# A decoder trunk on one Trainium2 core: tile addresses, a store queue, and the order of exponentials and scores

## The chip, the cores and the metric

The kernel runs on one core of one Trainium2 chip. The metric is the device time of one execution in microseconds (us), median of the runs shown. The core's engines run side by side, each in the order of its own queue: TensorE (PE in the profile, with PEld for its weight loads), VectorE (DVE), ScalarE (ACT), GpSimd (POOL) and SyncE (SP). They share the on-chip memories SBUF and PSUM. Transfers are issued by SP, ScalarE or POOL, each with a queue of its own, and carried out by 16 DMA engines.

## The reference, cut to what matters

A trunk of one layer over 512 tokens and 16 leading meta tokens, in float32. Two branches mix the tokens: causal pooling over four windows, and a Mamba-2 state-space branch (SSD) with 8 groups of 4 heads. Sigmoid gates merge them, and an MLP with a squared ReLU follows.

```python
proj = u @ w_in[i]                      # u = rmsnorm(h); columns: pool, z, xbc, dt, gates
xbc = jax.nn.silu(causal_depthwise_conv(xbc, conv_w, conv_b))
...
a_cs = jnp.cumsum(a_dt, axis=2)
lmat = jnp.exp(jnp.where(mask, a_cs[:, :, :, None] - a_cs[:, :, None, :], -jnp.inf))
cb = jnp.einsum("bclgn,bcsgn->bclsg", cf, bf)
y_diag = jnp.einsum("bclsg,bclsgr,bcsgrp->bclgrp", cb, lmat, xdt)
states = jnp.einsum("bclgn,bclgr,bclgrp->bcgrpn", bf, decay_states, xdt)
...
y_off = jnp.einsum("bclgn,bcgrpn,bclgr->bclgrp", cf, prev, jnp.exp(a_cs))
...
y_ssd = mamba2_branch(z, xbc, dt_raw, ...) @ w_ssd_out[i]
h = h + (gate_pool * y_pool + gate_ssd * y_ssd) @ w_o[i]
hid = jax.nn.relu(rmsnorm(h, mlp_norm_w[i]) @ w_ff1[i])
h = h + (hid * hid) @ w_ff2[i]
out = rmsnorm(h, final_norm_w)[:, N_META:]
```

The inputs are x, the meta tokens and the layer's weights; the output is 512 x 1024.

## The kernel before, in words

**Precision.** Every large product is computed as three products of halves: an operand is split into a high part (a rounding copy) and a low part (the rest), and hi·hi, hi·lo and lo·hi are summed in PSUM. A weight block of 128 x 1024 is loaded by SP into a tile `raw`, copied by ScalarE into `whi` (L94) and subtracted by VectorE into `wlo` (L96). `raw` has 3 buffers, `whi` and `wlo` have 4, all in the pool `wp`. Tiles whose names end in h and l are such halves: `uh`, `ul` of the normalised input, `yh`, `yl` of the SSD's result, `yph`, `ypl` of the pooling's, `vsh`, `vsl`, `vh`, `vl` and `hh`, `hl` in the MLP.

**Stages.** Up to some 70 us: the norm, group 0's projections and four gates. To some 500 us: a loop over the 8 groups g. Then the pooling branch (to some 560 us), the remaining gates with the merge and `w_o` (to some 700), and the MLP. Some products are computed by a scheme with seven products of quarter blocks in place of eight (`pair`, tiles `pqx`; in the pooling stage `pxx`, `py` and `pz` at L978; in the MLP `px` and `alpha`), which needs sums of weight blocks.

**The group loop.** In turn g the generator `ssd(g)` is woven with generators that fill PE's time: `group_proj(g + 1)` (the next group's projections), in turn 4 also `out_half` (the first half of the SSD's output projection, tiles `pso`), in turn 7 `out_part` (`psp`), and `weight_sums_at`.

`group_proj` makes, in this order, the projections for B and C (`px{g}_{16+g}`, `px{g}_{24+g}`), for the two halves of x (as `px{g}_{2g}` and `px{g}_{2g+1}`, or for the groups in `X_PAIRS`, 4 to 7, as one `pqx{g}`), a gate in some turns (`gate_pool`), and z (`pz`). `conv` turns a projection into the tile `bt`, `ct` or `xc`: a bias step on ScalarE that reads PSUM (L414), three steps on VectorE (L416, L417) and a silu on ScalarE (L419). PSUM has two buffers for the wide tiles and four for the small ones, so a projection waits for the bias step that frees its buffer. So `px7_23` is the projection for B of group 7, the first of the next group while `ssd(6)` runs.

`ssd(g)` is this: POOL loads `abc`, the running sums of the group broadcast over partitions (L572, issued on POOL's queue). PE transposes B into `ptb`, which ScalarE copies to `btok` (L581), and x into `ptm` and `ptx`, from which VectorE makes `xddm`, `xdt` and `xdd`. ScalarE takes the exponential of `abc` into `eb` in two halves (L603), and ScalarE and VectorE subtract and clip (L608 the ScalarE part); `decay` takes the exponentials of the rest (L614, L615). PE makes the scores `pcb` (L625), which VectorE masks into `cbm`, and the states `pst` (L632, L634) from `btok`. ScalarE copies the first state to `st` (L636), VectorE chains the others. VectorE multiplies the decays by the masked scores. PE makes `po` from `st` (L654) and `py` from the decays (L660). The result is normalised (`png`, `rs` at L681) and split into `yh` and `yl` (L690).

**Stores.** `gate_pool` writes gates 0 to 6 to DRAM (`gate_d`, L719) and `out_half` writes its sums (`acc_d`, L798); both are read back in the merge. They are issued on POOL's queue, as the load of `abc` and the weight sums are.

**Weight sums.** `weight_sums_at` forms sums of weight blocks by transfers alone, on POOL's queue, which add into DRAM: eight transfers in a set of `fx` or `f1`, four in one of `f2`. Ahead of each step POOL copies one element into `seen`, a 128 x 1 tile whose only purpose is to hold the step back until a certain point of the computation (`mark`). `SETS_AT` says how many sets run in each turn of the loop, `SETS_POOL` how many in the pooling stage; what is left runs at the start of the MLP. The sets are taken from one list in a fixed order, among them f1's third set (f12), f2's third and fourth (f22, f23), f1's fourth (f13) and f2's fifth (f24), in this order.

**What sets the order.** A scheduler orders each engine's instructions as the program is built, with costs of its own. `tc.issue_after(x)` adds an edge: what stands within it is put behind x in the same engine's queue; it adds no wait. Tiles get their addresses as their pools are opened: `const`, to which `seen` belongs, stands ahead of the other pools on the left side, so its size shifts them.

Of the kernel before, what the change touches and what calls it, by code (L numbers as in the profile page):

```python
# [9 lines left out]
F32 = mybir.dt.float32  # L10
F32R = mybir.dt.float32r
AF = mybir.ActivationFunctionType
ALU = mybir.AluOpType

P = 128
# [34 lines left out]
X_PAIRS = (4, 5, 6, 7)  # L50
BC_PAIRS = ()
PAIRS = [(k, g) for g in range(G) for k in "bx" if g in (BC_PAIRS if k == "b" else X_PAIRS)]

SETS_AT = {g: 1 for g in range(7)}
SETS_POOL = 3

PLAIN = 4

# [5 lines left out]
def kernel(ctx: ExitStack, tc, xT, x, w, fx, f1, f2, vec, fnw, out):  # L64
    nc = tc.nc
    act, dve, pe, pool = nc.scalar, nc.vector, nc.tensor, nc.gpsimd

    const = ctx.enter_context(tc.tile_pool(name="const", bufs=1, side="left"))
# [29 lines left out]
    def block(behind=None):  # L98
        t = block_tiles()
        block_load(t, slice(0, 1024))  # L100
        block_split(t, slice(0, 1024), behind)
        return t[2:]
# [45 lines left out]
    def col(off, i, n=P):  # L148
        return vs[:n, off + i : off + i + 1]
# [3 lines left out]
    dec = const.tile([P, 4, HEADS], F32, name="dec")  # L153
    cdec = const.tile([P, 4, HEADS], F32, name="cdec")
    wmeta = const.tile([P, HEADS], F32, name="wmeta")
    seen = const.tile([P, 1], F32, name="seen")
    dve.memset(wmeta, 0.0)

    u_stack = ExitStack()
# [12 lines left out]
    gate_d = [dram.tile([P, SEQ], F32, name=f"gate_d{d}") for d in range(NK)]  # L172
    acc_d = [dram.tile([P, SEQ], F32, name=f"acc_d{d}") for d in range(NK)]

    def psum2(name):
        return psa.tile([P, 1024], F32, tag="mm", name=name)

    def psum1(name):
        return psb.tile([P, 512], F32, tag="s", name=name)
# [10 lines left out]
    def proj(outs, wblk, rhs):  # L190

        for part in range(2):
            for k in range(NK):
                wt = wblk[part][:, k * P : (k + 1) * P]
                for o, c in outs:
                    pe.matmul(o, wt, rhs[0][k][:, c], start=part == 0 and k == 0, stop=part == 1 and k == NK - 1)  # L196
                    if part == 0:
                        pe.matmul(o, wt, rhs[1][k][:, c], start=False, stop=False)  # L198

    def wide(ps, skip=0):  # L200

        h = (L - skip) // 2
        runs = [(ps[:, 512 - h : 512], slice(skip, skip + h)),
                (ps[:, 512 : 512 + h], slice(skip + h, L))]
        return runs, ps[:, 512 - h : 512 + h]

    def narrow(ps):
        return [(ps, slice(NM, L))]
# [117 lines left out]
    for t, name in ((rsh, "dgh"), (rsl, "dgl")):  # L326
        d = pre.tile([NT, 6, NT], F32R, tag="sq", name=name, bufs=2)
# [3 lines left out]
    for i in range(2):  # L331
        pb = psum1(f"pb1_{i}")
        c = slice(3 * i, 3 * i + 3)
        for n in range(2):
            pe.matmul(pb[:, : 3 * NT], ones_r[:NT], dg[n][:, c, :].rearrange("p a b -> p (a b)"),
                      start=n == 0, stop=n == 1)
# [70 lines left out]


    mark, first_part = [None], [True]

    def conv(dst, src, ct):
        n = dst.shape[-1]
        e = src.shape[-1] - n
        act.activation(dst, src[:, e:], AF.Identity, bias=col(V_CB, ct), scale=col(V_CW, ct * 4 + 3))  # L414
        for j in range(1, 4):
            o = max(0, j - e)  # L416
            dve.scalar_tensor_tensor(dst[:, o:], src[:, e + o - j : e + n - j],  # L417
                                     col(V_CW, ct * 4 + 3 - j), dst[:, o:], op0=ALU.mult, op1=ALU.add)
        act.activation(dst, dst, AF.Silu)  # L419
        if first_part[0]:  # L420
            mark[0] = dst[:, :1]

    def group_tiles(g):
        xc = gc.tile([P, 2, L], F32, tag="xc", name=f"xc{g}")
        bt = gc.tile([P, L], F32, tag="bt", name=f"bt{g}")
        ct = gc.tile([P, SEQ], F32, tag="ct", name=f"ct{g}")
        zt = gc.tile([P, 2, SEQ], F32, tag="zt", name=f"zt{g}", bufs=1)
        return xc, bt, ct, zt

    def first_raw(name, ps, skip):  # L430
        r = pre.tile([P, L - skip], F32, tag="raw0", name=f"raw0_{name}", bufs=3)
        act.copy(r, ps)
        dve.tensor_tensor(r, r, rsb[:, skip:], op=ALU.mult)
        return r
# [65 lines left out]
    def raw_pair(kind, g):  # L500
        return [stg.tile([P, L], F32, tag=t, name=f"{t}{kind}{g}") for t in ("ra", "rb")]

    def group_proj(g, cur, gate=None):

        first = g == 0
        xc, bt, ct, zt = cur

        def plain(dst, t, skip):
            if first and (dst is bt or dst is ct):
                view = viewB if dst is bt else viewC  # L510
            else:
                runs, view = wide(psum2(f"px{g}_{t}"), skip)
                proj(runs, block(), X if first else U)
            conv(dst, first_raw(t, view, skip) if first else view, t)

        def z_half(ps, i):

            with tc.issue_after(done[0].ins) if g == 1 else nullcontext():
                wt = block()
            proj(narrow(ps), wt, X if first else U)  # L520

        bcs = ((bt, 16 + g, 0), (ct, 24 + g, NM - 4))
        xs = ((xc[:, 0, :], 2 * g, 0), (xc[:, 1, :], 2 * g + 1, 0))
        both = g in BC_PAIRS
        for kind, ts, paired in (("b", bcs, both), ("x", xs, g in X_PAIRS)):
            if paired:
                r = raw_pair(kind, g)
                yield from pair(kind, g, r)
                for (dst, t, skip), src in zip(ts, r):
                    conv(dst, src[:, skip:], t)  # L530
                yield
            else:
                for t in ts:
                    plain(*t)
                    yield
            if both:
                i = 0 if kind == "b" else 1
                ps = psum2(f"pz{g}_{i}")[:, :SEQ]
                z_half(ps, i)
                act.activation(zt[:, i, :], ps, AF.Silu)  # L540
                yield
        if both:
            return
        if gate is not None:
            gate_pool(gate)
            yield
        ps = psum2(f"pz{g}")
        for i in range(2):
            z_half(ps[:, i * SEQ : (i + 1) * SEQ], i)
        zf = zt.rearrange("p i t -> p (i t)")  # L550
        if first:
            dve.tensor_tensor(zt, ps.rearrange("p (i t) -> p i t", i=2),
                              rsb[:, NM:].unsqueeze(1).to_broadcast([P, 2, SEQ]), op=ALU.mult)
            act.activation(zf, zf, AF.Silu)
            mark[0] = zf[:, :1]
        else:
            act.activation(zf, ps, AF.Silu)
        yield
# [5 lines left out]
    def ssd(g, cur):  # L564

        xc, bt, ct, zt = cur
        hs = slice(R * g, R * g + R)
        tok = lambda c: slice(NM + c * P, NM + (c + 1) * P)
        ctok = lambda c: slice(c * P, (c + 1) * P)
# [17 lines left out]
        for b in range(2):  # L587
            pt = psum1(f"ptx{g}_{b}")
            for c in range(2):
                for i in range(2):  # L590
                    o = c * 256 + i * P
# [7 lines left out]
        eb = gs.tile([P, 2, SEQ], F32, tag="eb", name=f"eb{g}")  # L599
        ap = abc.rearrange("p (i j) l -> p i j l", j=2)  # L600
        for j in range(2):
            js = slice(64 * j, 64 * j + 64)
            act.activation(eb[js, :, :], ap[js, :, j, :], AF.Exp)  # L603
        dm = abc.rearrange("p r (c l) -> p r c l", c=4)
        for r in range(R):
            for c in range(4):
# [14 lines left out]
        yield  # L621

        pc = psum1(f"pcb{g}")
        for c in range(4):
            pe.matmul(pc[:, c * P : (c + 1) * P], bt[:, tok(c)], ct[:, ctok(c)], start=True, stop=True)  # L625
        cbm = gs.tile([P, 4, P], F32, tag="cbm", name=f"cbm{g}")
        dve.tensor_tensor(cbm, pc.rearrange("p (c l) -> p c l", c=4),
                          tri.unsqueeze(1).to_broadcast([P, 4, P]), op=ALU.mult)
# [4 lines left out]
        for c in range(3):  # L633
            pe.matmul(pv[c + 1], btok[:, c, :], xdd[:, c, :, :].rearrange("p r d -> p (r d)"),  # L634
                      start=True, stop=True)
# [75 lines left out]
    def gate_pool(d, first=False):  # L711
        ps = psum2(f"pgp{d}")[:, :SEQ]
        proj(narrow(ps), block(), X if first else U)
        o = m1[d] if d in m1 else staged(f"gp{d}")
        if first:
            dve.tensor_tensor(o, ps, rsb[:, NM:], op=ALU.mult)
        act.activation(o, o if first else ps, AF.Sigmoid, bias=col(V_BG, d))
        if d not in m1:
            nc.gpsimd.dma_start(gate_d[d], o)  # L719


    sets = [("fx", n) for n in range(fx.shape[0])] + [
# [68 lines left out]
    def out_half():  # L791
        for dd in range(4):
            ps = psum2(f"pso{dd}")
            for i in range(2):
                ssd_out(2 * dd + i, ps[:, i * SEQ : (i + 1) * SEQ], range(8))
                o = staged(f"so{2 * dd + i}")
                act.copy(o, ps[:, i * SEQ : (i + 1) * SEQ])
                nc.gpsimd.dma_start(acc_d[2 * dd + i], o)  # L798
                yield

    def out_part():
# [93 lines left out]
    for g in range(G):  # L895
# [4 lines left out]
        if g in SUMS_AT:  # L900
            fill.append(sums_of_u(SUMS_AT[g], g))
        for _ in range(SETS_AT.get(g, 0)):
            fill.append(weight_sums_at())
# [118 lines left out]
    for d in range(NK):  # L1022
        t_load = nc.gpsimd.dma_start(acc[d], acc_d[d])
    for _ in range(SETS_POOL):
        with tc.issue_after(t_load.ins):
# [582 lines left out]
    c = NC - 1  # L1608
# [14 lines left out]
    for t in range(4):  # L1623
        T, st = t // 2, slice((t % 2) * P, (t % 2 + 1) * P)
        n = 0
        for half in range(2):
            parts = [(0, 512)] if half == 0 or t < 3 else [(0, 256), (256, 256)]
            for a, m in parts:
# [3 lines left out]
                i = 0  # L1632
# [4 lines left out]
                for k, seg in ((1, (A11, 3)[T]), (0, (A12, A22)[T])):  # L1637
                    wh, wl = wq[k, half]
                    for p in range(2):
# [3 lines left out]
                        for lhs, rhs in ((hh, wh), (hh, wl), (hl, wh)):  # L1643
                            pe.matmul(ps, lhs[:, p, seg, st], rhs[:, x0 : x0 + m], start=f and lhs is hh and rhs is wh,
                                      stop=i == 4 and lhs is hl, skip_group_check=True)
# [166 lines left out]
```

## Time and profile before

| | us |
|---|---|
| median of 3 runs | 1041.87 |
| the runs | 1039.58, 1042.01, 1041.87 |
| the profiled execution | 1041.83 |
| its span, first to last instruction | 1040.1 |
| PE busy | 1011.5 |
| VectorE busy | 800.5 |
| ScalarE busy | 616.6 |
| POOL busy | 119.5 |

The profiled execution takes 1.7 us more than its span, which runs from the first to the last instruction. The mean clock that PE was granted in it is 0.988 of full speed.

How to read the views: a row of operations names the line of the kernel, the engine, the operation, and out<-in by the names of tiles without their numbers; then the shape and how many of them. For a matmul the first operand after the arrow is the one that streams and the second the one whose 128 x 128 blocks are loaded as weights. In a timeline the start and the busy time stand ahead (us), and in brackets the engine's idle time before it with what ended it. A wait is put down to the operation that ended last of those waited for. Ends of matmuls are modelled, so the pace of PE is better read from their starts.

### The profile page before, as it was taken

The page shows a single profiled execution, that of the slowest core. Times are in us where ns is not written, and L with a number is a line of the kernel's source. Part 1 is how long each engine was busy: PE and PEld are TensorE (multiplying, and loading weights), DVE is VectorE, ACT ScalarE, POOL GpSimd, SP SyncE. Part 2 cuts the span into 40 slices and gives each one's busy share as a digit, 9 for nine tenths or more (in the row PEclk, how much of TensorE's full clock was granted, in tenths as well). Part 3 has the DMA queues.
Part 4 walks back from the last instruction along what each step waited for, and adds up shares of the span by engine and source line. Part 5 has one row for each costly group of instructions (what it writes and reads, how often), then busy time and mean ns, then how long its engine had stood idle before and what let it go on. Part 6 is the DMA issues. An engine that isn't in the chain of part 4 may idle for free.

```text
span 1040.1 us, 15623 instructions
## 1 busy us (share of the span) xinstructions
PE 1011.5 (97%) x6047; PEld 881.4 (85%) x6047; DVE 800.5 (77%) x1153; ACT 616.6 (59%) x863; POOL 119.5 (11%) x196
## 2 busy tenths in 40 slices
PE   9998999999899998989989999999999999999997
PEld 7887998998688896977879888887889898998986
DVE  7966897978735776878569755876988888888885
ACT  7656859596726538495334533458655665665654
POOL 0430202112003002011421000221000000000000
PEclk9998999999999998999999999999999999999999
DMA  7693866546748627457897642779454455454432
GB/s 255 175 294 104 230 175 176 158 127 236 169 162 242 174 93 196 155 155 172 244 281 190 213 166 81 258 189 314 110 168 154 148 176 151 156 169 155 142 102 81
DMA packets 60330, 184.51 MB, mean 177 GB/s; under 512 B 7072, under 2 KB 8416, under 8 KB 59232
## 3 DMA queue, kind: packets, MB, share of 16 engines
q1 hardware_dynamic: 39456, 109.00, 31.6%
q0 software_dynamic: 20080, 73.61, 27.3%
q8 instruction: 47, 0.77, 0.3%
q10 hardware_dynamic: 720, 0.91, 0.3%
q14 instruction: 27, 0.22, 0.1%
HBM read 173.13 MB, written 58.59 MB: 223 GB/s over the span
## 4 chain that ended last, share of the span: by engine, by line
PE 73%; ACT 9%; DMA 7%; DVE 5%; issue 4%; POOL 1%; ACTq 0%; POOLq 0%; DVEq 0%; SPq 0%
PE px L1431 8%; PE alpha L1499 6%; PE px L196 6%; PE px L1434 4%; PE px L198 3%; PE alpha L1502 3%; PE pgs L196 3%; DMA raw<-in_w 2%; PE pz L196 2%; PE pqx L480 2%; PE pso L128 2%; PE py L660 2%; DMA abc<-acs_d 2%; PE pso L129 2%; PE po L654 2%
## 5 line engine op out<-in xcount | busy, mean ns | idle before, releaser
L96 DVE TENSOR_TENSOR wlo<-raw,whi 128x1024 fp32r<-128x1024 f32 (+2 forms) x90 | 104.9, 1172 | 42.7 <-ACT whi L94 30.0
L94 ACT CAST whi<-raw 128x1024 fp32r<-128x1024 f32 (+2 forms) x90 | 89.9, 1011 | 80.4 <-PE pso L129 16.9
L196 PE MATMUL px<-uh,whi 128*128 128x264 f32 (+1 forms) x320 | 82.2, 294 | 0.0
L198 PE MATMUL px<-ul,whi 128*128 128x264 f32 (+1 forms) x320 | 79.7, 287 | 0.0
L1206 DVE TENSOR_TENSOR ht<-ht,alpha 128x1024 f32<-128x1024 f32 x35 | 42.7, 1220 | 30.7 <-PE alpha L1499 30.7
L196 PEld LDWEIGHTS px<-uh,whi 128*128 128x128 f32 x320 | 61.4, 192 | 1.4 <-issue 0.9
L1129 ACT CAST shi<-rawf 128x1024 fp32r<-128x1024 f32 x42 | 44.0, 1048 | 29.3 <-PE alpha L1502 18.2
L198 PEld LDWEIGHTS px<-ul,whi 128*128 128x128 f32 x320 | 61.1, 191 | 0.3
L1499 PE MATMUL alpha<-shi,hh 128*128 128x512 f32 x140 | 55.4, 396 | 0.0
L1502 PE MATMUL alpha<-shi,hl 128*128 128x512 f32 x140 | 55.3, 395 | 0.0
L1130 DVE TENSOR_TENSOR slo<-rawf,shi 128x1024 fp32r<-128x1024 f32 x42 | 51.2, 1218 | 0.6 <-ACT shi L1129 0.6
L1431 PE MATMUL px<-vsh,shi 128*128 128x256 f32 x192 | 47.6, 281 | 0.0
L1434 PE MATMUL px<-vsl,shi 128*128 128x256 f32 x192 | 47.5, 281 | 0.0
L196 PE MATMUL pz<-uh,whi 128*128 128x512 f32 x112 | 43.9, 392 | 1.3 <-ACT yh L690 1.3
L198 PE MATMUL pz<-ul,whi 128*128 128x512 f32 x112 | 43.7, 390 | 0.0
L196 PE MATMUL px<-uh,wlo 128*128 128x264 f32 (+1 forms) x320 | 41.8, 283 | 0.0
L196 PEld LDWEIGHTS px<-uh,wlo 128*128 128x128 f32 x320 | 39.9, 188 | 0.0
L1499 PE MATMUL alpha<-slo,hh 128*128 128x512 f32 x140 | 38.3, 395 | 0.0
L1434 PEld LDWEIGHTS px<-vsl,shi 128*128 128x128 f32 x192 | 36.1, 188 | 1.1
L1431 PEld LDWEIGHTS px<-vsh,shi 128*128 128x128 f32 x192 | 36.1, 188 | 1.1
L1431 PE MATMUL px<-vh,shi 128*128 128x256 f32 x144 | 35.8, 281 | 0.0
L1434 PE MATMUL px<-vl,shi 128*128 128x256 f32 x144 | 35.7, 281 | 0.0
(599 smaller groups left out, 3092.2 us busy)
## 6 DMA issues: line engine op xcount, KB each, us to landing
raw<-in_w SPq DMA_DIRECT2D x96, 512.0 KB, 4.6
f_t<-in_f POOLq DMA_DIRECT2D x38, 512.0 KB, 7.8
f_s<-in_f POOLq DMA_DIRECT2D x26, 512.0 KB, 8.3
b<-in_f SPq DMA_DIRECT2D x21, 512.0 KB, 4.6
rawf<-in_f SPq DMA_DIRECT2D x36, 256.0 KB, 2.9
rawf<-f_t SPq DMA_DIRECT2D x36, 256.0 KB, 2.7
abc<-acs_d POOLq DMA_DIRECT2D x8, 1024.0 KB, 7.2
f_t<-f_t POOLq DMA_DIRECT2D x12, 512.0 KB, 6.5
```

Source lines behind the costliest of these rows:

```text
L94: act.copy(hi[:, c], raw[:, c])
L96: dve.tensor_tensor(lo[:, c], raw[:, c], hi[:, c].bitcast(F32), op=ALU.subtract)
L128: pe.matmul(ps, ah, bh, start=first and n == 0, stop=False)
L196: pe.matmul(o, wt, rhs[0][k][:, c], start=part == 0 and k == 0, stop=part == 1 and k == NK - 1)
L198: pe.matmul(o, wt, rhs[1][k][:, c], start=False, stop=False)
L1129: splits.append((act.copy(hi, src), dve.tensor_tensor(lo, src, hi.bitcast(F32), op=ALU.subtract)))
L1130: dve.tensor_tensor(lo, src, hi.bitcast(F32), op=ALU.subtract)))
L1206: added[0] = dve.tensor_tensor(o, o, src, op=op)
L1431: pe.matmul(ps, m, f[k][0], start=start and not low and k == 0, stop=stop and low == 1 and k == 3, skip_group_check=True)
L1434: pe.matmul(ps, m, f[k][1], start=False, stop=False, skip_group_check=True)
L1499: pe.matmul(ps[t], hh[:, p, seg, st], m, start=bool(first and not low and p == 0), stop=bool(last and low and p == 1), skip_group_check=True)
L1502: pe.matmul(ps[t], hl[:, p, seg, st], m, start=False, stop=False, skip_group_check=True)
```

## The change

Five things change.

- The tile `seen` is allocated 64 elements (256 bytes a partition) wide, of which one is used as before. By the addresses of the built program this moves the pool `wp` (`raw`, `whi`, `wlo`), `uh`, `ul`, the staging tiles and the MLP's residual from 0 to 224 modulo 256 bytes, and the sums of u (`T`) by as much; the tiles of the group loop go from 128 to 96, and some of the MLP's (`v32`, `vsl`'s pool) from 224 to 192. Those of the mixer's and the MLP's halves (`yh`, `yl`, `yph`, `vh`, `vl`, `hh`, `hl`) stay at 224.
- The stores of `gate_d` (7) and `acc_d` (8) are issued by ScalarE in place of POOL.
- The exponentials into `eb` stand behind x's silu of the same group (the second of the two) on ScalarE. The two halves of x have a silu each; `x_ready[g]` holds that of the second half. The scheduler puts it ahead of the other one in groups 5 to 7, and one of the two exponentials between them.
- The scores `pcb` of a group in `X_PAIRS` stand behind the last hi·lo matmul of the next group's first projection, where that is a plain one.
- One set of weight sums more runs in turn 4, one less in the pooling stage: f12 in turn 4, f22 and f23 in turns 5 and 6, f13 and f24 in the pooling stage.

In the built program PE, VectorE and SP issue the same instructions as before; ScalarE has 15 more transfers and three fewer loads of activation tables, POOL 15 transfers fewer and two copies into `seen` more. The scheduler moves a few things besides: in turn 4, `pcb4` and `pst4` stand behind the first 24 matmuls of `pso0`, and the casts of its first two weight blocks stand ahead of `xc4`'s bias step; in turn 5 the transposes of x stand behind the first of `px6_22`'s matmuls; in turn 6 the transposes of x stand among `px7_23`'s matmuls and `pcb6` and `pst6` behind all of them.

```diff
-SETS_AT = {g: 1 for g in range(7)}
-SETS_POOL = 3
+SETS_AT = {0: 1, 1: 1, 2: 1, 3: 1, 4: 2, 5: 1, 6: 1}
+SETS_POOL = 2
...
-    seen = const.tile([P, 1], F32, name="seen")
+    seen = const.tile([P, 64], F32, name="seen")[:, :1]
...
                     if part == 0:
-                        pe.matmul(o, wt, rhs[1][k][:, c], start=False, stop=False)
+                        mm[0] = pe.matmul(o, wt, rhs[1][k][:, c], start=False, stop=False)
+
+    mm = [None]
...
+    x_ready, filled = {}, {}
...
-        act.activation(dst, dst, AF.Silu)
+        silu = act.activation(dst, dst, AF.Silu)
         if first_part[0]:
             mark[0] = dst[:, :1]
+        if ct < 16:
+            x_ready[ct // 2] = silu
...
                 for t in ts:
                     plain(*t)
+                    filled.setdefault(g - 1, mm[0])
                     yield
...
         for j in range(2):
             js = slice(64 * j, 64 * j + 64)
-            act.activation(eb[js, :, :], ap[js, :, j, :], AF.Exp)
+            with tc.issue_after(x_ready[g].ins):
+                act.activation(eb[js, :, :], ap[js, :, j, :], AF.Exp)
...
-        for c in range(4):
-            pe.matmul(pc[:, c * P : (c + 1) * P], bt[:, tok(c)], ct[:, ctok(c)], start=True, stop=True)
+        with tc.issue_after(filled[g].ins) if g in X_PAIRS and g in filled else nullcontext():
+            for c in range(4):
+                pe.matmul(pc[:, c * P : (c + 1) * P], bt[:, tok(c)], ct[:, ctok(c)], start=True, stop=True)
...
         if d not in m1:
-            nc.gpsimd.dma_start(gate_d[d], o)
+            nc.scalar.dma_start(gate_d[d], o)
...
                 act.copy(o, ps[:, i * SEQ : (i + 1) * SEQ])
-                nc.gpsimd.dma_start(acc_d[2 * dd + i], o)
+                nc.scalar.dma_start(acc_d[2 * dd + i], o)
```

## The prediction

> **What bounds the kernel now.** I read the page first, then the waits of PE, then PE's granted clock and the other engines around each wait, and last the chains on ScalarE that end the waits.
>
> ```profile
> span 1040.1 us, 15623 instructions
> PE 1011.5 (97%) x6047; PEld 881.4 (85%) x6047; DVE 800.5 (77%) x1153; ACT 616.6 (59%) x863; POOL 119.5 (11%) x196
> ```
>
> PE sets the end: 97% of the span, so only two things can shorten it, PE's idle time and the pace of its matmuls. The waits of PE (total, times, longest, us):
>
> ```profile
> PE pst L632 <- ACT btok L581: 5.3, 2, 4.3
> PE po L654 <- ACT st L636: 3.5, 1, 3.5
> PE pso L128 <- ACT whi L94: 3.2, 1, 3.2
> PE pz L978 <- DVE wloB L115: 2.4, 1, 2.4
> PE pqx L480 <- DVE rbx L496: 1.5, 1, 1.5
> PE psp L840 <- ACT yh L690: 1.4, 1, 1.4
> PE pz L196 <- ACT yh L690: 1.3, 1, 1.3
> PE png L678 <- ACT qhg L308: 0.7, 1, 0.7
> PE py L660 <- issue: 0.6, 1, 0.6
> ```
>
> Almost all end on a ScalarE copy in the SSD stages: ScalarE is idle on average and late in a few places. By stretches (span in us; its length; busy us and count of PE, PEld, DVE, ACT, POOL; PE's granted clock; DMA share; GB/s):
>
> ```profile
> 64.00:72.00 8.00, 8.00 (x44) 6.68 (x42) 3.34 (x4) 1.06 (x2) 3.30 (x7) 1.00 0.98 295
> 72.00:81.00 9.00, 9.00 (x71) 8.79 (x70) 4.39 (x7) 2.25 (x3) 1.63 (x3) 1.00 1.02 407
> 86.40:91.30 4.90, 0.80 (x3) 0.53 (x3) 2.39 (x2) 4.90 (x9) 0.00 (x0) 0.78 0.00 0
> 91.30:96.00 4.70, 4.70 (x28) 4.31 (x29) 4.70 (x10) 3.01 (x4) 0.00 (x0) 0.50 0.00 0
> 266.60:275.60 9.00, 4.82 (x32) 3.76 (x30) 4.76 (x8) 8.94 (x15) 1.17 (x3) 1.00 0.51 72
> 275.60:280.30 4.70, 4.70 (x14) 3.71 (x15) 4.70 (x5) 2.09 (x3) 0.00 (x0) 0.64 0.74 155
> 349.50:387.00 37.50, 37.50 (x280) 34.22 (x278) 28.37 (x40) 14.75 (x20) 0.00 (x0) 1.00 0.31 98
> 406.60:415.30 8.70, 4.43 (x17) 3.46 (x17) 5.38 (x7) 8.61 (x10) 1.61 (x2) 0.69 0.52 80
> 415.30:417.00 1.70, 1.70 (x10) 1.70 (x9) 1.70 (x3) 1.70 (x4) 0.00 (x0) 0.55 0.82 157
> 540.80:545.00 4.20, 1.25 (x4) 0.94 (x4) 3.84 (x7) 1.05 (x1) 0.71 (x2) 0.77 0.95 278
> 545.00:550.00 5.00, 4.99 (x23) 4.99 (x24) 4.99 (x7) 1.33 (x2) 1.77 (x4) 0.51 0.91 212
> 580.22:585.67 5.45, 5.45 (x25) 4.50 (x24) 3.37 (x6) 1.84 (x3) 0.00 (x0) 1.00 0.57 178
> 588.47:594.06 5.59, 5.59 (x25) 4.51 (x24) 4.52 (x5) 3.53 (x4) 0.00 (x0) 1.00 0.24 59
> ```
>
> Four idle stretches (86, 270, 410, 541 us) are each followed by several us of half clock: the idle time is paid again. In the first three ScalarE is busy throughout (4.90 of 4.90, 8.94 of 9.00, 8.61 of 8.70).
>
> **The change part by part**, against the profiled execution (1041.83 us, beside the median of 1041.87).
>
> *Stores on ScalarE's queue; the first group.* The load of abc0 is issued by POOL, behind a gate_d store that waits for a gate (timeline of POOL, then the chain of waits, then the timeline of ScalarE):
>
> ```profile
> 65.38 0.84 POOL L719 DMA_DIRECT2D gate_d<-gp  x1
> 70.92 0.54 POOL L719 DMA_DIRECT2D gate_d<-gp  x1 [4.69 <-ACT gp L717]
> ...
> 71.45 9.53 DMA abc<-acs_d
> ...
> 82.37 2.15 ACT L603 ACTIVATE eb<-abc 64x1024 f32<-64x1024 f32 x2
> 84.54 2.45 ACT L608 ACTIVATE abc<-abc,dtok 128x128 f32<-128x128 f32 x8
> 89.46 0.35 ACT L636 COPY st<-pst 128x256 f32<-128x256 f32 x1
> ```
>
> abc0 lands at 71.45 + 9.53 = 80.98; the copy that PE waits for ends at 89.81, 8.8 us of ScalarE work later. Without the stores POOL would issue abc0 at about 65.4, and with the same flight it lands at 75; the DMA engines are full until 81 (0.98, 1.02), so it may land as late as today. The copy must end by 86.4, so 77.6 is late enough. Removable: 3.5 + 0.6 idle, plus (1 − 0.50) × 4.70 = 2.3 of half clock, 6.4 in all; between 0 and 6.4 I take 5.0, since 75 is well ahead of 77.6. The other stores wait on POOL for the gate or the copy before them, on ScalarE they follow it.
>
> Fifteen stores cost ScalarE their issue. The nearest row is its stores of the output (ns, min/median/max):
>
> ```profile
> L1525 ACTq DMA_DIRECT2D out_dram<-out x4: 341/346/348, 1022.5 to 1036.5; - x4
> ```
>
> 15 × 0.35 = 5.2 us. At 59% busy ScalarE hides most; without that cover all 5.2 would fall on PE. Eight of them stand between casts of out_half's weights, behind which PE queues: 1.0 taken, 0 to 5.2 kept.
>
> The Trainium skill says in "DMA: Bandwidth & Descriptors", under Issuing engines are not separate DMA queues, that transfers from any engine share the same 16 DMA engines, so another issuer saves only the issuing time. By that rule alone the first group gains nothing while those engines are full, and the sum is 5.0 us higher; the trace speaks for a gain all the same, since the 4.69 us is a wait of the issuing queue.
>
> *Exponentials behind x's silu; scores behind the next first projection.* In group 4 (timelines of PE and ScalarE):
>
> ```profile
> 270.16 0.70 PE L632 MATMUL pst<-xddm,btok 128*128 128x256 f32 x2 [0.99 <-ACT btok L581]
> 270.83 1.56 PE L634 MATMUL pst<-xdd,btok 128*128 128x256 f32 x6
> 275.58 0.50 PE L128 MATMUL pso<-yh,whi 128*128 128x512 f32 x1 [3.19 <-ACT whi L94]
> 274.50 1.98 ACT L94 CAST whi<-raw 128x1024 fp32r<-128x1024 f32 x2
> ```
>
> The casts stand behind the exponentials. In the built order of the changed kernel they stand before xc4's bias step, and pso0's first 24 matmuls stand ahead of pcb4 on PE: 24 × 5.59/24 = 5.6 us of ready work in front of the wait. Saved: 0.99 + 3.19, and (1 − 0.64) × 4.70 = 1.7 of half clock: 5.9.
>
> In group 6:
>
> ```profile
> 411.99 1.22 PE L632 MATMUL pst<-xddm,btok 128*128 128x256 f32 x2 [4.27 <-ACT btok L581]
> 413.01 2.77 PE L634 MATMUL pst<-xdd,btok 128*128 128x256 f32 x6
> 420.04 2.09 PE L196 MATMUL px<-uh,wlo 128*128 128x264 f32 x16
> ```
>
> px7_23 (415.30 to 422) moves ahead of pcb6 and pst6 and covers the copy. Saved: 4.27 of idle time, and the slow clock behind it: the eight pst matmuls take 3.3 us here (411.99 to 415.30) and 2.2 in group 4 (270.16 to 272.39), 1.1 more, and (1 − 0.55) × 1.70 = 0.8 follows. That is 6.2. Against it stands a new wait for xc6's second silu, which the built order puts behind half of the exponentials, at 2.15/2 = 1.1 us at most: 0.8 taken, so 5.4.
>
> Groups 2, 5 and 7: png 0.7, pz 1.3 and psp 1.4 each wait for a ScalarE cast that the built order puts ahead of what delays it now: 3.4. pqx (1.5, DVE) stays. What is delayed in turn is the chain of eb, relus and decays, 2.15 + 2.45 and twice 1.04, 6.7 us, that DVE's masks and py wait for. In group 5 it now runs behind x's silu, between zt5 and bt6's eviction; PE, DVE and SP have the same instructions as before, so only this order can make new waits. Taken as covered (bounds 0 and what the last rival prices).
>
> *One weight-sum set earlier.* f12's eight transfers move from the pooling stage to group 4, and f22, f23 follow one place up. They run on POOL's queue, ahead of the load of abc6, which scores and exponentials of group 6 wait for: between 349.5 and 387 POOL has nothing to do and the DMA share is 0.31, so they fit. In the pooling stage the wait for wloB (2.4, then (1 − 0.51) × 5.00 = 2.5 of half clock and some 1.0 at 0.77 before) sits at a DMA share of 0.95. With one set less it may go: between +0 and −5.9; 0 taken, since two sets are still there and the load competes with the kernel's own weights.
>
> *Addresses.* Making `seen` 256 bytes wide moves weight tiles (raw, whi, wlo), uh and ul from 0 to 224 modulo 256; the mixer's yh, the MLP's hidden and v tiles are at 224 already. Here the two 512-wide stretches of 24 matmuls differ: the one with uh and whi, both at 0, takes 5.45/24 = 227 ns a matmul, the one with yph (224) and whi (0) 5.59/24 = 233. The groups by form show the same 6 ns in their means:
>
> ```profile
> L196 PE MATMUL pz<-uh,whi 128*128 128x512 f32 x112 | 43.9, 392 | 1.3 <-ACT yh L690 1.3
> L1499 PE MATMUL alpha<-shi,hh 128*128 128x512 f32 x140 | 55.4, 396 | 0.0
> ```
>
> Over all such groups, some 660 matmuls are of the first kind and some 1570 of the second; after the change all have both operands at 224, which no row shows. If the difference of the two addresses decides, 1570 × 5.8 ns = 9.1 us are gained; if any address off 0 costs the same once, 660 × 5.8 = 3.8 are lost; if each operand pays, 660 × 11.6 + 1570 × 5.8 = 16.8. I take +3.8, the middle case: the 227 is seen only at 0. DVE and ScalarE show no such difference: 0.
>
> The Trainium skill ("TensorE: Matmul & The Clock Gate", Step-by-step: what each phase is for) gives PE two independent read ports, so that loading weights doesn't take from the streamed operand. By that rule addresses are worth nothing and the sum is 3.8 lower; the two stretches disagree by 5.8 ns.
>
> **Sum:** −5.0 − 5.9 − 5.4 − 3.4 = −19.7; + 1.0 (stores' issue) + 3.8 (addresses) = −14.9. 1041.83 − 14.9 = 1026.9, say 1027.
>
> **The rivals.**
> - *All operands in phase.* Addresses gain 9.1 instead of losing 3.8: 1027 − 12.9 = 1014. For it: 227 is seen only where both are equal; against: only at 0.
> - *Half the waits come back.* abc0 lands late again (DMA full) and the 6.7 us chain makes DVE the releaser where ScalarE was: 9.8 of the 19.7 are lost, 1037.
> - *Each operand pays for its address.* +16.8 instead of +3.8: 1040, no change. Against it: yph beside whi has one off 0, and a group with both off 0 is missing.
> - *Slower: the exponentials come too late.* Behind x's silu the 6.7 us chain holds ScalarE's evictions, PSUM isn't freed and PE waits in every following group. Each such wait costs its length and half as much clock behind it, as at 411 (4.3 and 1.9). At 4 us in each of six groups that is 6 × 6 = 36 against 14.9: 1063; it decides from 2.5 us a group, idle time and slow clock together (6 × 2.5 = 15). For it: ScalarE is full in just these stretches. Against: PE then runs the next projection, 6.6 us long (415.3 to 422). At the likeliest size, 4 in each of four groups, 1051.
> - *The change does nothing there:* the built order shows the instructions moved, so this is in the second rival.
>
> **How the numbers follow.** The forecast 0.55 (1020 to 1034: 1027 with the bounds of group 0, the stores and the pooling stage, not all on one side), in phase 0.18, half the waits 0.08, each operand 0.07, late exponentials 0.12. 0.3% is 3.1 us, what this measurement can tell from none: faster means under 1038.7, slower over 1045. Faster: 0.55 + 0.18 + 0.06 + 0.01 = 0.80; same: 0.02 + 0.05 = 0.07; slower: 0.01 + 0.12 = 0.13. The range leaves out the late exponentials and the best part of the in-phase case: 1012 to 1041.
>
> **What would show it.** Right: no wait of PE over 1 us on btok, st or whi, the half clock gone at 91, 276 and 412 us, abc0 landed by 78. The addresses: pgs's stretch of 24 at 227 (in phase), 233 (as taken) or 239. Wrong: new waits of PE on DVE's masks or on px evictions in groups 5 to 7; the wait at pz L978 longer, or f12's transfers delaying abc6.

## The result, and the profile after

| | us |
|---|---|
| before, median of 6 runs | 1039.61 |
| changed, median of 6 runs | 1027.96 |
| ratio, with its 95% interval | 0.9886 (0.9860 to 0.9912) |
| the changed kernel's profiled execution | 1029.08, span 1027.4 |

The forecast was 1027. The time is right; the two largest groups of terms behind it are not, as the rest shows, so the agreement is luck.

The page of the changed kernel, its first two rows:

```profile
span 1027.4 us, 15622 instructions
PE 1001.4 (97%) x6047; PEld 881.5 (86%) x6047; DVE 798.1 (78%) x1153; ACT 611.9 (60%) x860; POOL 111.8 (11%) x183
```

PE's work became 10.1 us shorter (1011.5 to 1001.4) with the same 6047 matmuls; only the rest of the 12.7 us between the spans can be idle time. After the first 20 us, PE's gaps of more than 0.1 us come to 18.3 us, against 21.4 before. The waits of PE in the changed kernel (total, times, longest, us):

```profile
PE ptm L590 <- ACT xc L422: 5.7, 1, 5.7
PE po L662 <- DVE st L650: 3.5, 3, 1.7
PE pdt L240 <- DVE ones_r L139: 1.5, 1, 1.5
PE po L662 <- ACT st L644: 1.4, 1, 1.4
PE pz L196 <- ACT yh L698: 1.3, 1, 1.3
PE pxx L986 <- ACT pu L992: 1.1, 1, 1.1
PE pst L640 <- ACT btok L587: 1.0, 1, 1.0
PE py L668 <- issue: 1.0, 1, 1.0
```

The four long waits of before are gone or smaller: on btok in group 6 (4.3), on whi in group 4 (3.2), on st in group 0 (3.5, now 1.4), on wloB in the pooling stage (2.4). In their place stand a wait of 5.7 us for x's silu and three on `st` by VectorE, two of them in group 3. By stretches (span in us; its length; busy us and count of PE, PEld, DVE, ACT, POOL; PE's granted clock; DMA share; GB/s):

```profile
88.00:94.00 6.00, 4.18 (x31) 3.77 (x32) 6.00 (x11) 4.40 (x5) 0.00 (x0) 0.82 0.00 1
226.00:243.00 17.00, 13.27 (x88) 11.61 (x89) 14.84 (x26) 12.48 (x20) 0.00 (x0) 0.87 0.20 52
360.50:369.20 8.70, 3.04 (x24) 2.75 (x22) 4.89 (x9) 6.72 (x8) 0.81 (x1) 0.95 0.74 155
369.20:376.00 6.80, 6.80 (x35) 6.80 (x36) 3.55 (x8) 6.75 (x13) 0.00 (x0) 0.57 0.10 20
572.91:578.35 5.44, 5.44 (x26) 4.51 (x24) 4.84 (x8) 1.83 (x3) 0.00 (x0) 1.00 0.39 111
581.07:586.51 5.44, 5.44 (x26) 4.51 (x24) 4.56 (x5) 3.52 (x4) 0.00 (x0) 1.00 0.29 82
```

The second row is group 3, 17 us with 3.7 idle; the third and fourth are group 5, 5.7 idle and then a clock of 0.57 over 6.8 us. The last two are one stretch of 24 matmuls of `pgs` and one of `pup`: both take 5.44/24 = 227 ns a matmul, where before it was 227 and 233.

The 5.7 us in group 5, from ScalarE's and SP's timelines of the changed kernel:

```profile
348.43 1.02 SPq L466 DMA_DIRECT2D rawp<-in_fx  x2
...
360.43 1.05 ACT L94 CAST whip<-rawp 128x1024 fp32r<-128x1024 f32 x1 [5.12 <-DMA rawp<-in_fx]
361.39 0.82 ACT L417 ACTIVATE xc<-rax,vs 128x528 f32<-128x528 f32 x1
...
368.45 0.64 ACT L422 ACTIVATE xc<-xc 128x528 f32<-128x528 f32 x1
```

ScalarE stands 5.1 us before a cast whose load is late; the bias step of `xc5` stands behind that cast, its silu ends at 369.1, and PE waits for it. The wait is put down to ScalarE; the cause is a load. Two stretches on either side, first before, then changed:

```profile
340.00:350.00 10.00, 8.71 (x61) 7.61 (x60) 7.34 (x11) 5.49 (x10) 0.81 (x1) 1.00 0.82 201
350.00:360.00 10.00, 10.00 (x59) 8.47 (x58) 7.13 (x10) 4.80 (x7) 0.00 (x0) 1.00 0.51 165
```

```profile
340.00:350.00 10.00, 8.74 (x58) 7.50 (x57) 6.36 (x10) 4.33 (x7) 3.54 (x7) 1.00 1.02 285
350.00:360.00 10.00, 10.00 (x56) 8.58 (x56) 4.24 (x5) 3.11 (x4) 0.81 (x1) 1.00 1.06 295
```

The DMA engines, half idle at 350 to 360 us before, are full there now. The weight set f12 runs exactly where SP fetches the operands of group 5's x.

### The profile page after: what moved, and what is told of

It reads as the page before. It is cut to its first block, busy times and chain, and to the rows that moved or that the text cites. A ratio compares the mean times of both kernels' runs of the same rounds, so it can differ in the third digit from the quotient of the medians.

```text
span 1027.4 us, 15622 instructions
## 1 busy us (share of the span) xinstructions
PE 1001.4 (97%) x6047; PEld 881.5 (86%) x6047; DVE 798.1 (78%) x1153; ACT 611.9 (60%) x860; POOL 111.8 (11%) x183
## 4 chain that ended last, share of the span: by engine, by line
PE 80%; DMA 6%; DVE 5%; ACT 5%; issue 3%; POOL 1%; SPq 0%; ACTq 0%; DVEq 0%; POOLq 0%
PE px L1439 8%; PE alpha L1507 6%; PE px L196 6%; PE px L1442 4%; PE px L198 3%; PE alpha L1510 3%; PE pz L196 3%; PE pgs L196 3%; PE pqx L485 2%; PE po L662 2%; DMA rawp<-in_fx 2%; PE py L668 1%; PE pso L128 1%; PE pz L198 1%; PE pso L129 1%
## 5 line engine op out<-in xcount | busy, mean ns | idle before, releaser
L1137 ACT CAST shi<-rawf 128x1024 fp32r<-128x1024 f32 x42 | 44.2, 1052 | 28.7 <-PE alpha L1510 18.3
```

The lines of the kernel that those rows point to most:

```text
L1137: splits.append((act.copy(hi, src), dve.tensor_tensor(lo, src, hi.bitcast(F32), op=ALU.subtract)))
```

## The experiments

Each ratio is to the kernel before, with its 95% interval.

### The addresses, three ways

The changed kernel with `seen` as before (`u_seen`), the kernel before with `seen` wide and nothing else (`b_seen`), and the changed kernel with `seen` half as wide (`seen32`). None of them moves an instruction on any engine; built, they differ from the kernel that they start from in addresses alone.

```diff
u_seen   -seen = const.tile([P, 64], F32, name="seen")[:, :1]
         +seen = const.tile([P, 1], F32, name="seen")
b_seen   -seen = const.tile([P, 1], F32, name="seen")
         +seen = const.tile([P, 64], F32, name="seen")[:, :1]
seen32   -seen = const.tile([P, 64], F32, name="seen")[:, :1]
         +seen = const.tile([P, 32], F32, name="seen")[:, :1]
```

> The change with `seen` 4 bytes wide again, so that wp, uh and ul lie at 0 modulo 256; the order on every engine is that of the changed kernel. Theory 1 (operands in phase): a 512-wide matmul takes 227 ns where both addresses agree modulo 256 and 233 where they differ. Then pgs (0, 0) stays at 227, pup, pso, pf and alpha go back from 227 to 233, some 1570 matmuls, and the run is 9.3 us slower than the changed kernel, about 1.1 to 1.3% of a gap to before shrinks to some 0.3%: ratio to before near 0.997. Theory 2 (the pace has another cause, as less traffic on the queues): all stay at 227 and the ratio is that of the changed kernel, 0.989.

> The kernel before with `seen` 256 bytes wide and nothing else; the order on every engine is that of before. Theory 1 (in phase): pup, pso, pf and alpha go from 233 to 227 ns, 1570 x 5.9 = 9.3 us faster, ratio 0.991, the idle times of PE at 90, 276, 412 and 543 us as before. Theory 2: 1.000. If both operands at 224 cost more than one, as the prediction had it, pgs would go to 233 and the ratio be 1.004.

> The change with `seen` 128 bytes wide: raw, whi, wlo, uh and ul lie at 96 modulo 256, the mixer's and the MLP's halves at 224 as before. Theory 1 (in phase modulo 256): pgs and pz (96 beside 96) take 227 ns, pup, pso, pf and alpha (224 beside 96) 233, so the run is about 8 us slower than the changed kernel, ratio 0.997. Theory 2 (in phase modulo 128 or less): all take 227, ratio 0.989. Theory 3 (0 and 224 are good places in themselves, not their agreement): pgs goes to 233 too, ratio 1.000.

| run | whi at | pgs (uh, whi) | pup (yph, whi) | median, us | ratio |
|---|---|---|---|---|---|
| u_seen | 0 | 0, 0 | 224, 0 | 1035.73 | 0.9968 (0.9952 to 0.9985) |
| b_seen | 224 | 224, 224 | 224, 224 | 1032.46 | 0.9931 (0.9904 to 0.9959) |
| seen32 | 96 | 96, 96 | 224, 96 | 1036.20 | 0.9964 (0.9943 to 0.9985) |

A stretch of 24 matmuls of `pgs`, and the 24 of `pup` behind it, in u_seen, b_seen and seen32:

```profile
588.85:594.32 5.47, 5.47 (x26) 4.51 (x25) 2.94 (x4) 1.36 (x2) 0.00 (x0) 1.00 1.00 395
594.32:599.92 5.60, 5.60 (x26) 4.51 (x24) 1.83 (x2) 2.69 (x3) 0.00 (x0) 1.00 0.66 225
```

```profile
587.47:592.91 5.44, 5.44 (x26) 4.51 (x25) 2.94 (x4) 2.41 (x3) 0.00 (x0) 1.00 0.98 395
592.91:598.35 5.44, 5.44 (x26) 4.51 (x25) 1.83 (x2) 1.74 (x2) 0.00 (x0) 1.00 0.86 313
```

```profile
585.30:590.75 5.45, 5.45 (x25) 4.51 (x24) 2.94 (x4) 2.26 (x3) 0.00 (x0) 1.00 1.00 397
590.75:596.34 5.59, 5.59 (x25) 4.50 (x24) 1.83 (x2) 1.89 (x3) 0.00 (x0) 1.00 0.73 287
```

Where the two operands agree (0 with 0, 224 with 224, 96 with 96) the second figure, the stretch's length, is 5.44 to 5.47; where they differ (224 with 0, 224 with 96) it is 5.59 to 5.60. So it is the difference of the two addresses that counts and not the place, and 224 and 96, which are 128 apart, count as different. A period longer than 256 isn't needed: in b_seen yph lies at 480 modulo 512 and whi at 224, and the pace is 227 all the same. The column of DMA share goes from 0.66 to 1.00 between rows and moves nothing. The Trainium skill's two independent read ports ("TensorE: Matmul & The Clock Gate", Step-by-step: what each phase is for) would have left all six alike, since by it the load of the weights takes nothing from the streamed operand; the trace disagrees by 6 ns in 227.

The address alone is worth 0.9931, some 7 us. Without it the change keeps 0.9968, some 3.4 us: that is all that stores, exponentials, scores and weight sums bring together.

### The weight sums

`u_sets` puts the sets back: f12 into turn 5, f22 into turn 6 and f23 into the pooling stage (f12 was in turn 5 before, not in the pooling stage as the prediction and the expectation below have it). PE, VectorE, ScalarE and SP keep the changed kernel's order. `sets2` also leaves one more set for the start of the MLP.

```diff
-SETS_AT = {0: 1, 1: 1, 2: 1, 3: 1, 4: 2, 5: 1, 6: 1}
+SETS_AT = {g: 1 for g in range(7)}
-SETS_POOL = 2
+SETS_POOL = 3   (u_sets; sets2 keeps 2)
```

> The change with the weight sums where they were before (f12 in the pooling stage); PE, ScalarE, VectorE and SP keep the order of the changed kernel. Theory 1 (f12's transfers in turn 4 make SP's loads of rawp land late): the idle 5.7 us of PE before ptm5 at 369 us and the 6.8 us of half clock behind it go, 9 us; the wait at pz L986 in the pooling stage (2.4 idle, 3.4 for the clock) comes back; the sum is 3 us faster than the changed kernel, ratio 0.986. Theory 2 (the exponentials behind x's silu are what is late there): the idle 5.7 us stays and the pooling stage loses 6, ratio 0.994.

> As the run with the weight sums where they were, but with two sets in the pooling stage, so that one set more is left for the start of the MLP. Theory 1: neither the idle time at 369 us nor the one in the pooling stage, 9 us faster than the changed kernel, ratio 0.980. Theory 2: the idle time at 369 us stays, and the pooling stage is as in the changed kernel, ratio 0.989. If the MLP waits for its first sums, the rows of its first product show a wait on a DMA and some of it is given back there.

Measured: u_sets 1023.89 us, 0.9857 (0.9830 to 0.9884); sets2 1020.69, 0.9827 (0.9796 to 0.9858). Waits of PE in u_sets, then its stretches:

```profile
PE pz L986 <- DVE wloB L115: 1.5, 1, 1.5
...
PE ptm L590 <- ACT xc L422: 0.7, 1, 0.7
```

```profile
340.00:350.00 10.00, 8.74 (x59) 7.50 (x58) 6.32 (x10) 4.34 (x7) 0.81 (x1) 1.00 0.66 168
350.00:360.00 10.00, 10.00 (x56) 8.60 (x56) 8.08 (x10) 6.39 (x8) 0.00 (x0) 1.00 0.57 177
360.00:368.80 8.80, 8.80 (x71) 8.47 (x70) 4.42 (x12) 8.71 (x15) 0.00 (x0) 1.00 0.00 0
```

With f12's transfers gone the DMA share falls from 1.06 to 0.57, PE is busy throughout (8.80 of 8.80) and group 5's wait for the silu, 5.7 us, is gone (the 0.7 left under that name stands at 405 us, in group 6), although the exponentials stand where the change put them. The wait in the pooling stage comes back at 1.5. The set in turn 4 thus costs more than it saves. The forecast that `sets2` shows no wait in the pooling stage missed: there `pz` waits 1.7 us, and it is fastest all the same.

### The exponentials

`u_exp` drops the edge in all groups, `exp_n3` in group 3 alone. The scheduler then moves other rows too: some 110 on PE in u_exp, 14 in exp_n3.

```diff
-            with tc.issue_after(x_ready[g].ins):
+            with tc.issue_after(x_ready[g].ins) if g != 3 else nullcontext():   (exp_n3; u_exp: no edge)
                 act.activation(eb[js, :, :], ap[js, :, j, :], AF.Exp)
```

> The change without the edge that puts the exponentials behind x's silu; the rest as changed. Theory 1 (the edge brings groups 4 and 6 what the prediction said, and costs group 3 a stall): the idle 1.0 and 3.2 us at group 4 and the 4.3 at group 6 come back with their half clock, 11 us, the idle 1.0, 0.5, 1.7 and 1.0 us of group 3 with 3.4 of half clock go, 7.6, and the 5.7 idle and 3.4 for the clock in group 5 stay as they hang on f12: 4 slower than the changed kernel, ratio 0.992. Theory 2 (the stall in group 5 is the exponentials' too): it goes as well, 5 faster, ratio 0.984.

> The change without the edge in group 3 alone: the first of group 3's two exponentials goes back ahead of x's second silu; ScalarE's order differs in some 20 rows. Theory 1 (the exponential and its table load behind the silu make ScalarE late for btok and VectorE's chain): the idle 1.0, 0.5, 1.7 and 1.0 us of PE at 227 to 240 and 3.4 us of half clock shrink to under 1 us, 6 us faster, ratio 0.983. Theory 2 (VectorE is late for rbu, the second load of u's sums, which POOL issues at 208 and which lands at 215.8 against 213.0 before): the idle times stay at 3 us or more, and the ratio at 0.988.

Measured: u_exp 1034.17 us, 0.9954 (0.9938 to 0.9971); exp_n3 1030.10, 0.9918 (0.9887 to 0.9950). The waits of PE in u_exp, then PE around the first of them and the stretch about it:

```profile
PE px L196 <- ACT whi L94: 8.2, 1, 8.2
PE po L661 <- ACT st L643: 5.9, 1, 5.9
PE ptm L590 <- ACT xc L422: 3.7, 1, 3.7
```

```profile
410.05 0.66 PE L598 MATMUL ptx<-ident,xc 128*128 128x128 f32 x4
418.92 0.59 PE L196 MATMUL px<-uh,whi 128*128 128x264 f32 x1 [8.22 <-ACT whi L94]
412.00:424.00 12.00, 5.08 (x27) 5.08 (x28) 9.27 (x12) 9.74 (x12) 0.00 (x0) 0.57 0.14 44
```

Without the edge the schedule is slower, by more than theory 1 had, but not by the waits it named: group 4's on btok and whi stay away, and group 6's comes back as one of 8.2 us for a weight cast, with a granted clock of 0.57 over 412 to 424. Group 0's wait on `st`, 5.9, is longer too. Of the 5.7 us for the silu in group 5 3.7 remain; theory 1 had all of it staying, but that wait is 4.1 in seen32, which keeps the changed kernel's order, so its size varies. The edge is worth some 6 us (1034.17 against 1027.96), with the edge on the scores in place; that one is taken up below.

In group 3 (exp_n3) the wait on btok goes and those on VectorE's `st` stay:

```profile
PE po L662 <- DVE st L650: 2.1, 2, 1.4
PE pqx L485 <- DVE rbx L501: 1.5, 1, 1.5
```

That is 0.7 and 1.4 us of idle time in place of 4.2, with another 1.5 us for `rbx` at 258, and nothing is won in time. The 2.1 lie between the two theories (under 1, 3 or more), so the order of the exponentials has a part in this stall; what sets off the rest, the next run shows.

### Group 3: the loads of u's sums

The chain to group 3's late states begins on POOL. VectorE at that place, in the changed kernel:

```profile
215.96 0.43 DVE L874 TENSOR_TENSOR rbu<-rau,rbu 128x264 f32<-128x264 f32 x1 [8.49 <-DMA rbu<-u_d]
```

`rbu` is the second of two loads for the sums of u. In the changed kernel POOL's order has the weight sums of turn 2 between and ahead of the two (issued 208.00, landed 215.84); before, the first of the two stood ahead of the weight sums and the second landed at 212.99. Its issue is no later than before (208.34 there): the flight is 7.8 us in place of 4.7, with a weight sum's transfer issued just ahead of it. `sets2_late` is `sets2` with those sums put behind the loads; four rows of POOL's order move and nothing else.

```diff
-                    nc.gpsimd.dma_start(t, u_d[kk])
+                    u_loaded[0] = nc.gpsimd.dma_start(t, u_d[kk])
...
-            at = pool.tensor_copy(seen, mark[0])
+            with tc.issue_after(ahead[0].ins) if ahead[0] is not None else nullcontext():
+                at = pool.tensor_copy(seen, mark[0])
...
-            fill.append(weight_sums_at())
+            fill.append(later(weight_sums_at(), 6) if g == 2 else weight_sums_at())
```

`later` lets six steps of the weave pass and then sets `ahead[0] = u_loaded[0]` for the generator's steps.

> The run with two sets in the pooling stage (1020.7), and in turn 2 the weight sums of that turn stand behind the loads of u's sums on POOL's queue; four rows of POOL's order differ, the other engines keep theirs. Theory 1 (group 3's stall hangs on rbu): rbu is issued at some 206 and lands by 211 in place of 216, VectorE is no longer idle 8 us before it, and of the 4 us of idle time of PE at 227 to 240 and the 3.4 us its half clock costs at least 4 us go: ratio 0.979. Theory 2 (it hangs on ScalarE's order of the exponentials): no change, 0.983.

Measured: 1014.47 us, 0.9767 (0.9751 to 0.9784), some 6 us under `sets2`. VectorE in it:

```profile
205.07 1.22 DVE L96 TENSOR_TENSOR wlo<-raw,whi 128x1024 fp32r<-128x1024 f32 x1
210.16 0.43 DVE L882 TENSOR_TENSOR rbu<-rau,rbu 128x264 f32<-128x264 f32 x1 [3.87 <-DMA rbu<-u_d]
```

The load lands 5.8 us earlier, and of group 3's idle time 0.3 us is left, with no half clock behind. The idle time of PE after the first 20 us is 8.4 us, over gaps of more than 0.1 us, against 21.4 before. It is the fastest of all versions here.

What the stall costs hangs on the clock behind it. In u_sets the same four waits make 4.2 us, as in the changed kernel, but the granted clock stays at 1.00 from 226 to 248 us; in the changed kernel it is 0.95 over 226 to 240 and 0.66 over 240 to 248. With the stores on POOL the same edit is worth 1.9 us alone (1018.97 to 1017.09 in the next table). So the 6 us are the upper end.

### The stores

`u_store` issues the fifteen stores from POOL in the changed kernel, `sets2_store` in `sets2`, `sets2_late_store` in `sets2_late`. The scheduler moves some 25 rows on PE and as many on VectorE with them.

```diff
-            nc.scalar.dma_start(gate_d[d], o)
+            nc.gpsimd.dma_start(gate_d[d], o)
...
-                nc.scalar.dma_start(acc_d[2 * dd + i], o)
+                nc.gpsimd.dma_start(acc_d[2 * dd + i], o)
```

> The change with the stores of gate_d and acc_d on POOL's queue again. Theory 1 (the move brings the first group 5 us, as the prediction had it): abc0 is issued some 5 us later, at about 71, lands at 81, and PE waits 3.5 and 0.6 us at 90 with half clock behind; ratio 0.993. Theory 2 (the 16 DMA engines are full until 81 us whoever issues, so an earlier issue lands no sooner): abc0 lands between 79 and 82 in both, the first group is unchanged within 2 us, and what the move does lies elsewhere, in the order on POOL and ScalarE: ratio 0.987 to 0.991.

> The run with two sets in the pooling stage (1020.7), with the stores of gate_d and acc_d on POOL's queue again. If the move of the stores is worth something of its own, this is slower: by 3 to 5 us if it is the first group's load of abc0, ratio 0.987. If it is worth nothing or less, because abc0 lands no sooner and ScalarE's issues cost it some, the ratio is 0.980 to 0.983.

> Both of the last: u's sums ahead in turn 2, and the stores on POOL's queue. If both theories hold (rbu sets group 3's stall, the stores' queue is worth nothing) this is the fastest or level with the better of the two, ratio 0.978 to 0.981; if the stores' move is worth 3 to 5 us, it is slower than the run with u's sums ahead by that much.

| stores on | ScalarE, us | POOL, us | POOL, ratio |
|---|---|---|---|
| changed kernel | 1027.96 | 1024.64 | 0.9874 (0.9840 to 0.9907) |
| sets2 | 1020.69 | 1018.97 | 0.9809 (0.9794 to 0.9825) |
| sets2_late | 1014.47 | 1017.09 | 0.9790 (0.9773 to 0.9808) |

The sign differs between the rows and the intervals overlap, so the move is worth nothing that these runs can settle, and not the 3 to 5 us of the forecast. Nor do the first two rows price it alone: with the stores on POOL that queue has both loads of u's sums ahead of most of turn 2's weight sums, and group 3 waits 2.0 us in place of 4.2 (changed kernel) and 3.6 (sets2). The line is the same in u_store and sets2_store:

```profile
PE po L662 <- DVE st L650: 2.0, 1, 2.0
```

In the third row the loads are ahead in both, and there ScalarE's queue is 2.6 us the better. The load of abc0, start and flight, from the chains of waits of the changed kernel, u_sets (in both the stores are on ScalarE) and u_store (on POOL):

```profile
65.39 13.71 DMA abc<-acs_d
```

```profile
65.98 15.88 DMA abc<-acs_d
```

```profile
71.36 10.23 DMA abc<-acs_d
```

They land at 79.1, 81.9 and 81.6; before it was 81.0. Issued 6 us earlier, the load is under way 4 to 6 us longer. The Trainium skill's rule ("DMA: Bandwidth & Descriptors", Issuing engines are not separate DMA queues) holds here to within 2 us.

### The edge on the scores

It was not run by itself, because in the changed kernel there is nothing to run: built without it, that kernel has the same order on every engine. The scores of groups 4 and 6 stand where they do by the scheduler's own choice, which the edge on the exponentials moves. In `u_exp`, where that edge is missing, the one on the scores does act: it puts `pcb6` and `pst6` behind all of `px7_23`, whose weight cast is the one that PE waits 8.2 us for; built without either edge, they stand ahead of it as before. A kernel with neither edge was not run, so what the two are worth together is open.

## Why the prediction was right, and where it was not

**The time was right by luck: two errors cancel.** The prediction had −18.7 from waits (−19.7 and the stores' +1.0) and +3.8 from addresses. Measured, everything but the addresses is worth −3.4 (`u_seen`), and the addresses −6.7 to −7.8 (`b_seen` against before, the changed kernel against `u_seen`). Of the signs that it named, the half clock is gone at 276 and 412 us, but not at 91; abc0 lands at 79.1, not by 78; and waits on btok and st of 1.0 to 1.7 us remain. The rival "half the waits come back" pointed the right way: abc0 is late again, as it said, but the other waits that came stand in groups 3 and 5, and hang on loads that it didn't name.

**Addresses: the wrong case was taken.** "If any address off 0 costs the same once" is refuted by the 24 matmuls at 96 and at 224, which take 227 ns, and "each operand pays" with it. The rival "all operands in phase" was right in mechanism, and near in size: by the starts of all matmuls before and in `b_seen`, some 1640 went from 233 to 228 ns on average, 8.6 us, and the 256-wide ones gave back 0.5. The reason noted against it, that 227 was seen only at 0, could not tell the two apart: at 0 both operands had been at 0, and no pair in that trace agreed elsewhere among the 512-wide ones in long use. The price of 5.8 ns was right.

**Group 0, −5.0: mis-sized.** The step was that the load "with the same flight lands at 75". It lands at 79.1. The lower bound of the same paragraph, full DMA engines, was the right end. The idle time fell from 4.1 to 3.2 us (1.40, 0.95 and 0.87), the half clock behind it from 6.8 to 3.4 us; but in `u_sets`, with the same order there, the wait on `st` is 3.6 again, and in `b_seen`, with the stores still on POOL, it is 2.0, so this much varies from run to run.

**Groups 4 and 6, −5.9 and −5.4: right in size, in part by another cause.** No wait of over 1 us is left in either, and the clock is whole behind them. Group 6's gain hangs on the edge on the exponentials: in `u_exp` a wait comes back there in another form. Group 4's doesn't: its long waits stay away in `u_exp`, without the edge, and in `u_store`, with the stores on POOL, and the kernel before, built with nothing but the stores moved, has the 24 matmuls of `pso0` ahead of `pcb4` too. Either of the two changes brings that order, so its 5.9 can't be put down to one. The 0.8 taken for xc6's second silu isn't there in the changed kernel and is 0.7 in `u_sets`.

**Groups 2, 5 and 7, −3.4: mis-sized.** The wait on png went, 0.7; `pz` still waits 1.3 for yh; `psp`'s 1.4 became 0.7 and 0.5. That is 0.9 of the 3.4. pqx's 1.5, which was to stay, became 0.5 and 0.2.

**New waits, "taken as covered": wrong, and not from the chain that the prediction watched.** By itself the exponentials' chain makes none of size, though it adds to group 3's (2.1 of the 4.2 us stay without it). POOL's queue makes two. The step "so they fit" for f12 failed: it was read from the DMA share over 349.5 to 387, 0.31, while the set's transfers go out between 329 and 365 and meet SP's loads at 340 to 360. It cost 5.7 us of idle time and half clock behind. The set's origin was wrong as well: POOL's rows before have f12 in turn 5, from 392.9 to 413.5 us; what leaves the pooling stage is f23, with four transfers. And the loads of u's sums in turn 2, which the change doesn't name, fell behind the weight sums in POOL's order: 4.2 us and the half clock at 238.6. `sets2_late` against `sets2` prices the second at 6 us, `sets2_late_store` against `sets2_store` at 1.9; `u_sets` against the changed kernel the first at 4, after what the pooling stage gives back.

**Pooling stage, 0: mis-sized.** The wait for wloB went, with its half clock, some 5 us, near the bound of −5.9. `sets2`, which has as many transfers there and waits 1.7, shows that it isn't the set's going alone; what decides it is open.

**The slower rival** (late exponentials in four to six groups) is refuted: with the two loads out of the way, in `sets2_late`, no wait of PE in groups 4 to 7 is longer than 1.3 us.

## What to carry to other kernels

Read each operand's address beside the other's: 512-wide matmuls here ran some 2.5% faster where both agree modulo 256 bytes, and padding one tile that stands ahead of a pool moves every tile of that pool. When a transfer is moved into a gap of the DMA engines, take the gap from the microseconds in which it will be in flight, and name the loads that are in flight there too; the wait that it causes shows up under the name of a compute engine. An edge in a scheduler's order moves things that it doesn't name: list the other queues' order, POOL's among them, before pricing it at nothing.

## What the runs showed of the hardware

The pace of a matmul with a 512-wide moving operand hangs on the agreement of its two operands' addresses modulo 256: 227 ns at (0, 0), (96, 96) and (224, 224), 233 at (224, 0) and (224, 96). The MLP's 256-wide ones don't gain by it (by form 281 ns on average before, 280 to 283 in `b_seen`). The same idle time was not followed by the same clock: behind the 4.2 us of group 3 it was 0.66 over 240 to 248 us in the changed kernel and 1.00 in `u_sets`. And an issue 6 us earlier into full DMA engines (a share of 0.92 over 64 to 72 us and 1.02 over 72 to 81) brought a load that landed at most 2 us earlier.
